# Layer-0 adaLN parts as column-tiled products, and attention outputs in two column halves

## The chip, the cores and the metric

The kernel runs on one core of one Trainium2 chip. Its metric is the device time of one execution in microseconds (us), the median of several runs. Engine names: TensorE (PE; its weight loads are shown as PEld), VectorE (DVE), ScalarE (ACT), GpSimd (POOL), SyncE (SP, which here only starts loads).

## The reference

The model is a trunk of two layers on 512 latent tokens and 256 context tokens of width 1024. What matters here is layer 0: its adaLN parameters and its neighbourhood attention.

```python
silu_c = jax.nn.silu(c)
silu_cc = jax.nn.silu(c_ctx)
for i in range(DEPTH):
    mod_lat = (silu_c @ ada_w[i] + ada_b[i])[:, None, :]
    mod_ctx = (silu_cc @ ada_w[i] + ada_b[i])[None, None, :]
    sh1, sc1, g1, sh2, sc2, g2 = jnp.split(mod_lat, 6, axis=-1)
    csh1, csc1, cg1, csh2, csc2, cg2 = jnp.split(mod_ctx, 6, axis=-1)
    h_lat = modulate(rmsnorm(x, norm_g[i, 0]), sh1, sc1)
    ...
    x = x + g1 * rmsnorm(y_lat, norm_g[i, 1])
    h = modulate(rmsnorm(x, norm_g[i, 2]), sh2, sc2)
...
p = jax.nn.softmax(jnp.concatenate([s_nb, s_cx], axis=-1), axis=-1)
o = (jnp.einsum('bhrqk,brkhd->brqhd', p_nb, v_blk)
     + jnp.einsum('bhrqc,bchd->brqhd', p_cx, v_ctx))
```

Two conditioning vectors, one for latent tokens and one for context tokens, are multiplied with a 1024 x 6144 matrix per layer. The context tokens have an attention of their own with the same keys and values (`context_attention`, 8 heads of width 64).

## The kernel before

Most products run as three fp32r products of split operands (a high and a low part). The stages of layer 0 are the setup and first normalization, spatial gating (`sgu`), attention, the output projection with the residual, and the MLP (`ffn`); layer 1 has retention and a second MLP.

**adaLN.** Four pieces of the first shift and scale are made at the start by `ada_first` (L166): four blocks of 128 rows of the matrix are multiplied side by side, the conditioning vectors as stationary operand 32 columns wide (`c32`), each in its own group of 32 output partitions. The remaining twelfths of layer 0 and all of layer 1, called halves (512 columns of the 6144), are made by `ada_half` (L233). A half loads four blocks of weights (512 KB each, tag `raw`, three buffers shared with other weights). VectorE multiplies each weight row by its conditioning value and adds into an accumulator per stream (latent, context): 8 operations a stream. The accumulators `acc` start from a memset by GpSimd and the bias row, loaded on GpSimd's queue. They are then split, and TensorE sums over the partitions: for gates with a matrix of ones (`ag`), after which VectorE multiplies by the norm weights into a gate tile; for shifts and scales with a selector (`ac`), a copy of the two rows, and four small transposes (`at`).

These halves are generators. `self.bg()` (L220) advances the first of the list `self.jobs` by one step; a step ends at a `yield`. `sgu` calls it six times, `attention` three times while it projects the first pair of heads, and then at every second tile of its loop (L810-811). Layer 0's list (L1693) holds halves 4 and 5 (the attention gate) and 6 to 9 (shift and scale of the MLP). Halves 10 and 11 are made in the MLP stage.

**Attention.** `attention` (L762) walks over 40 tiles, 8 heads with 5 tiles each: four of 128 latent queries, and one of the 256 context queries. For a tile, `score` (L902) makes the scores on TensorE, and VectorE and ScalarE make the softmax. Two tiles later `weigh` (L968) transposes the weights (`pt`, 128 x 512) and ScalarE copies them (`pt_all`, or `pcT` for the context). After the fourth latent tile of a head, six fp32 products with the values (`o`, 64 output partitions, 512 query columns) follow at once; after the context tile, two (`oc`, 256 columns). ScalarE and VectorE split the outputs out of PSUM into `at`. Between these stand the projections of the next pair of heads (`fills`).

PSUM tiles have tags: A with four banks, B with two (scores), C with two. C serves `pt`, `o`, `oc`, the transposed values `vn`, and the adaLN tiles. TensorE, like each engine, works through its queue in order; the order of the queues is set by a scheduler that follows the program's order as priority.

Of the kernel before, what the change touches and what calls it, by code (L numbers as in the profile page):

```python
# [8 lines left out]
F32 = mybir.dt.float32  # L9
# [4 lines left out]
ALU = mybir.AluOpType  # L14
AX = mybir.AxisListType

P = 128
# [51 lines left out]
class Trunk:  # L69
# [66 lines left out]
    def setup(self):  # L136
# [10 lines left out]
        self.ng = self.const("ng", [P, 64], a["ng_col"])  # L147
        self.ones = self.cp.tile([P, P], F32R, name="ones", tag="ones")
# [84 lines left out]
    def ada_half(self, l, half, streams, gate=None, away=False, fine=False):  # L233
        S, V, T, G = self.S, self.V, self.T, self.G
        m, h = divmod(half, 2)
        acc = []
        for s in range(streams):
            t = (self.lp if s else self.bp).tile([P, 512], F32, name=f"acc{l}{half}{s}", tag=f"acc{s}", bufs=1)
            G.memset(t, 0.0)
            G.dma_start(t[0:1], self.a["adab_row"][l * 12 + half : l * 12 + half + 1])  # L240
            acc.append(t)
# [65 lines left out]


# [453 lines left out]
    def attention(self, y, final):  # L762
        a = self.a
        with ExitStack() as ctx:
# [7 lines left out]
            n, lag = len(tiles), 2  # L772
# [8 lines left out]
            for i in range(n + lag):  # L781
# [23 lines left out]
                if i >= lag:  # L805
                    h2, b2 = tiles[i - lag]
                    self.weigh(h2, b2, pairs[h2 // 2], heads[h2])
# [160 lines left out]
    def weigh(self, h, b, pr, hd):  # L968

        S, V, T = self.S, self.V, self.T  # L970
        pt_all, sc = self.pt_all, hd[b]
        rows = slice(64 * (h % 2), 64 * (h % 2) + 64)
        at = pr["at"]
        vc = lambda i: pr["vn"][:, i, rows]
        pt = self.ps(f"pt{h}{b}", "C", (P, 4, P))
        if b < 4:
            for i in range(4):
                T.transpose(pt[:, i, :], sc[:, i * P : (i + 1) * P], self.ident)
            S.copy(pt_all[:, b], pt)
            if b < 3:  # L980
                return
            po = self.ps(f"o{h}", "C")[:64]
            flat = pt_all.rearrange("p a b q -> p (a b) q")
            T.matmul(po, vc(4), pt_all[:, :, 2, :], start=True, stop=False)
            T.matmul(po, vc(5), pt_all[:, :, 3, :], start=False, stop=False)
            T.matmul(po[:, 0:256], vc(1), flat[:, 1:5:3, :], start=False, stop=False)
            T.matmul(po[:, 128:384], vc(2), flat[:, 5:9:3, :], start=False, stop=False)
            T.matmul(po[:, 256:512], vc(3), flat[:, 9:14:4, :], start=False, stop=False)
            T.matmul(
                po.rearrange("p (a q) -> p a q", a=4)[:, 0:4:3, :], vc(0), flat[:, 0:13:12, :], start=False, stop=True  # L990
            )
            src = po.rearrange("p (a r l) -> p r a l", a=4, r=8)
            ov = [x[rows, 0:512].rearrange("p (r a l) -> p r a l", r=8, a=4) for x in at]
            self.split(ov[0], ov[1], src)
            return
        s2 = sc.rearrange("p (b c) -> p b c", b=2)
        for kt in range(2):
            for i in range(2):
                T.transpose(pt[:, 2 * kt + i, :], s2[:, i, kt * P : (kt + 1) * P], self.ident)
        pcT = self.t2k(f"pcT{h}")  # L1000
        S.copy(pcT, pt.rearrange("p k q -> p (k q)"))
        po = self.ps(f"oc{h}", "C")[:64, 0:256]
        for kt in range(2):
            T.matmul(po, vc(4 + kt), pcT[:, kt * 256 : kt * 256 + 256], start=(kt == 0), stop=(kt == 1))
        self.split(at[0][rows, 512:768], at[1][rows, 512:768], po)


# [657 lines left out]
    def build(self):  # L1665
# [19 lines left out]
        with ExitStack() as ctx:  # L1685
# [7 lines left out]
            self.jobs = [self.ada_half(0, h, 2, g1) for h in (4, 5)] + [self.ada_half(0, h, 2) for h in (6, 7, 8, 9)]  # L1693
# [132 lines left out]
```

## Time and profile before

| | |
|---|---|
| median of 3 runs | 1916.56 us (1914.06 to 1920.36) |
| profiled execution, its own time | 1919.05 us |
| its span | 1917.3 us |
| TensorE clock granted, mean | 0.975 |
| HBM read and written | 191.81 MB, 39.85 MB |

The profile is of one execution. A row of a timeline gives start, duration, engine, line, operation, the written and the read tiles, shape and count. Durations of TensorE records include the way through the array, so successive records overlap; what an instruction occupies is read from start to start. All rows carry line L61, because a helper there records every operation; tiles tell the rows apart. A row of waits gives the waiting engine and tile, whom it waited for, the total, the count and the longest.

### The profile page before, as it was taken

Reading aid. Unit: us, or ns where it says so; the run is one execution under the profiler, and the core shown is the slowest. Engines: PE = TensorE matmul, PEld = TensorE weight load, DVE = VectorE, ACT = ScalarE, POOL = GpSimd, SP = SyncE. Lnnn points to the kernel's source line nnn. Section 1 sums busy time; section 2 is a strip of 40 time slices with the busy share of each in tenths; the row PEclk is TensorE's granted clock in tenths of the full one; section 3 lists DMA queues with packets and bytes.
Section 4 is the critical chain, followed back from the end, with each engine's and each line's share of the span. In section 5 each row is a group of like instructions: output and inputs, shape, how many; then the busy total and the mean of one; then the engine's idle time right before and its main releaser. Section 6 shows DMA issues by size and latency. Waiting matters only on the chain. (4 is left out here: it accounts for less than half of the span.)

```text
span 1917.3 us, 28690 instructions
## 1 busy us (share of the span) xinstructions
PE 1799.9 (94%) x10928; PEld 1600.1 (83%) x10928; DVE 1397.0 (73%) x2334; ACT 1019.0 (53%) x1822; POOL 338.7 (18%) x471
## 2 busy tenths in 40 slices
PE   6998989889999999999979999999999989999997
PEld 4886767569989899998869889988999779889986
DVE  4834777779977777877877666676655689788877
ACT  4523545666555555555565434434444467566763
POOL 2102223130122222222021110011001100122221
PEclk9998989989999999999999999999999989999999
DMA  8323332232577778776633413331421225777773
GB/s 309 116 72 105 94 102 72 70 129 69 178 169 154 178 153 171 145 166 138 232 137 121 125 49 113 110 104 51 132 67 56 99 72 154 186 183 181 185 174 101
DMA packets 83978, 250.31 MB, mean 131 GB/s; under 512 B 11136, under 2 KB 12672, under 8 KB 83840
## 3 DMA queue, kind: packets, MB, share of 16 engines
q1 hardware_dynamic: 56960, 199.00, 31.6%
q0 software_dynamic: 26304, 49.36, 15.3%
q8 instruction: 86, 1.41, 0.3%
q14 instruction: 52, 0.43, 0.1%
q10 hardware_dynamic: 576, 0.11, 0.0%
HBM read 191.81 MB, written 39.85 MB: 121 GB/s over the span
## 5 line engine op out<-in xcount | busy, mean ns | idle before, releaser
L61 DVE SCALAR_TENSOR_TENSOR acc<-ar,cs,acc 128x512 f32<-128x512 f32 x256 | 189.5, 758 | 48.4 <-DMA ar<-in_adaw 27.6
L61 DVE SCALAR_TENSOR_TENSOR cv<-pre,cw,cv 128x769 f32<-128x769 f32 (+1 forms) x176 | 152.5, 880 | 7.9 <-ACT cv L61 7.4
L61 ACT ACTIVATE cv<-pre,cw 128x770 f32<-128x770 f32 (+1 forms) x88 | 81.0, 923 | 39.9 <-DVE pre L61 39.1
L61 POOL DMA_DIRECT2D yf<-yp x64 | 54.4, 850 | 269.8 <-ACT yp L61 238.6
L61 POOL DMA_DIRECT2D yd<-yp x54 | 45.9, 862 | 194.0 <-ACT yp L61 187.6
L61 ACT COPY yp<-wf 128x512 f32<-128x512 f32 x118 | 67.9, 577 | 21.2 <-PE wf L61 20.8
L61 ACT ACTIVATE pre<-px 128x256 f32<-128x256 f32 (+2 forms) x160 | 54.3, 365 | 44.7 <-PE px L61 44.3
L61 POOL DMA_DIRECT2D yd<-ypg x54 | 44.7, 851 | 155.4 <-ACT ypg L61 152.9
L61 POOL TENSOR_SCALAR rrr<-rmv 128x2 f32<-128x2 f32 x16 | 3.0, 190 | 357.2 <-DVE rmv L61 357.2
L61 ACT ACTIVATE g<-cv 128x770 fp32r<-128x770 f32 (+1 forms) x44 | 32.5, 738 | 28.2 <-DVE cv L61 28.0
L61 PE MATMUL px<-hs,wd 128*128 128x384 f32 x240 | 45.4, 337 | 0.3 <-DVE pre L61 0.3
L61 PEld LDWEIGHTS px<-hs,wd 128*128 128x128 f32 x240 | 42.3, 188 | 2.2 <-DVE pre L61 0.8
L61 DVE TENSOR_TENSOR g<-cv,g 128x770 fp32r<-128x770 f32 (+1 forms) x44 | 36.1, 821 | 7.2 <-ACT g L61 6.6
L61 ACT ACTIVATE pre<-py 128x384 f32<-128x384 f32 (+1 forms) x40 | 17.4, 436 | 44.5 <-DVE cv L61 25.4
L61 DVE TENSOR_TENSOR pre<-pre,pz 128x256 f32<-128x256 f32 (+1 forms) x60 | 20.8, 370 | 26.1 <-PE pz L61 25.9
L61 ACT ACTIVATE cv<-cv 128x770 f32<-128x770 f32 (+1 forms) x44 | 32.7, 743 | 13.0 <-DVE cv L61 12.9
L61 POOL TENSOR_TENSOR tm<-slab,mask 128x256 f32<-128x256 f32 (+1 forms) x32 | 29.6, 954 | 54.3 <-DVE sst L61 54.2
L61 PEld LDWEIGHTS px<-hs 128*128 128x128 f32 x240 | 32.0, 197 | 8.0 <-DVE pre L61 6.9
L61 PE MATMUL px<-hs 128*128 128x256 f32 x240 | 33.6, 291 | 5.1 <-DVE pre L61 5.1
L61 ACT ACTIVATE sc<-sc,sst 128x512 f32<-128x512 f32 x32 | 23.0, 720 | 28.1 <-DVE sc L61 28.0
L61 DVE TENSOR_TENSOR cv<-cv 128x770 f32<-128x770 f32 (+1 forms) x44 | 36.1, 821 | 2.5 <-ACT cv L61 1.5
L61 ACT COPY ypg<-wf 128x512 f32<-128x512 f32 x54 | 30.8, 577 | 8.8 <-PE wf L61 8.7
(2607 smaller groups left out, 6859.2 us busy)
## 6 DMA issues: line engine op xcount, KB each, us to landing
ar<-in_adaw SPq DMA_DIRECT2D x96, 512.0 KB, 4.2
yf<-yp POOLq DMA_DIRECT2D x64, 256.0 KB, 4.0
yd<-yp POOLq DMA_DIRECT2D x54, 256.0 KB, 5.0
yd<-ypg POOLq DMA_DIRECT2D x54, 256.0 KB, 4.7
fin<-xd SPq DMA_DIRECT2D x10, 512.0 KB, 6.3
xd<-xd SPq DMA_DIRECT2D x8, 512.0 KB, 3.3
xn<-in_x SPq DMA_DIRECT2D x6, 512.0 KB, 8.1
ngr<-in_norm_g POOLq DMA_DIRECT2D x12, 256.0 KB, 3.8
```

Of the source, the lines that this page charges most:

```text
L61: r = f(*p, **k)
```

## The change

1. `ada_packed` takes the place of `ada_half` for the six halves of layer 0 that run in `sgu` and `attention`. TensorE multiplies the weights in fp32, four blocks of 128 rows side by side in four column groups of 32, twice. ScalarE copies the packed result, and the bias row is loaded into partition 2 of the copy. For gates, a full-width fp32 product with a selector (`rows`, made in the setup) sums the groups and the bias; for shifts and scales, four transposes and a sum on VectorE do it. A gate half has four steps and a tail, a shift or scale half three and a tail.
2. The accumulators of the halves that stay with `ada_half` are in the pool of their stage.
3. The value products of a head are five pairs, the left 256 queries in output partitions 0 to 63 and the right 256 in 64 to 127; the context products are two pairs of 128 queries. Each half is split out separately.
4. `weigh` returns these products, and the loop issues them one tile later, before the next transposes.

```diff
+        self.rows = []
+        for i in range(2):
+            v = self.cp.tile([P, 1], F32, name=f"rowv{i}", tag=f"rowv{i}")
+            V.tensor_reduce(
+                out=v, in_=self.ident.rearrange("p (j c) -> p c j", j=4)[:, i, :], axis=AX.X, op=ALU.add
+            )
+            V.tensor_tensor(out=v, in0=v, in1=self.ident[:, 2:3], op=ALU.add)
+            row = self.cp.tile([P, P], F32, name=f"row{i}", tag=f"row{i}")
+            V.tensor_copy(row, v.broadcast_to([P, P]))
+            self.rows.append(row)
...
-            t = (self.lp if s else self.bp).tile([P, 512], F32, name=f"acc{l}{half}{s}", tag=f"acc{s}", bufs=1)
+            t = self.xp.tile([P, 512], F32, name=f"acc{l}{half}{s}", tag=f"acc{s}", bufs=1)
...
+    def ada_packed(self, l, half, streams, gate=None, away=False):
+        S, V, T, G = self.S, self.V, self.T, self.G
+        m, h = divmod(half, 2)
+        ps = self.ps(f"ad{l}{half}", "C")
+        for pair in range(2):
+            for kp in (2 * pair, 2 * pair + 1):
+                raw = self.bp.tile([P, 1024], F32, name=f"ar{l}{half}{kp}", tag="raw", bufs=3)
+                self.load(raw, self.ada_unit_src(l, half, kp))
+                for kk in range(2):
+                    k = 2 * kp + kk
+                    j = k % 4
+                    T.matmul(
+                        ps[32 * j : 32 * j + 32],
+                        self.c32[:, k, :],
+                        raw[:, kk * 512 : kk * 512 + 512],
+                        start=(pair == 0),
+                        stop=(pair == 1),
+                    )
+            yield
+        mr = self.t2k(f"mr{l}{half}")
+        S.copy(mr, ps)
+        G.dma_start(mr[2:3], self.a["adab_row"][l * 12 + half : l * 12 + half + 1])
+        ngr = None
+        if m in (2, 5):
+            ngr = self.t2k(f"ngr{l}{half}")
+            row = l * 4 + (1 if m == 2 else 3)
+            G.dma_start(ngr, self.a["norm_g"][row : row + 1, h * 512 : h * 512 + 512].broadcast_to([P, 512]))
+        yield
+        if m in (2, 5):
+            for s in range(streams):
+                pg = self.ps(f"ag{l}{half}{s}", "C")
+                T.matmul(pg, self.rows[s], mr, start=True, stop=True)
+                dst = gate[s][:, h * 512 : h * 512 + 512]
...
+                    V.tensor_tensor(out=dst, in0=pg, in1=ngr, op=ALU.mult)
+                if s == 0:
+                    yield
+            return
+        pt = self.ps(f"at{l}{half}", "C", (P, 4, P))
+        for i in range(4):
+            T.transpose(pt[:, i, :], mr[:, i * P : (i + 1) * P], self.ident)
+        md = self.bp.tile([P, 4, 2], F32, name=f"md{l}{half}", tag="mt", bufs=2)
+        V.tensor_reduce(out=md, in_=pt.rearrange("p b (j c) -> p b c j", j=4)[:, :, 0:2, :], axis=AX.X, op=ALU.add)
...
+        V.tensor_tensor(out=to, in0=md.rearrange("p b s -> p s b"), in1=two(pt[:, :, 2]), op=ALU.add)
+        if m not in (0, 3):
+            V.scalar_tensor_tensor(
+                out=to, in0=to, scalar=1.0, in1=two(self.ng[:, gi : gi + 4]), op0=ALU.add, op1=ALU.mult
+            )
...
-            for i in range(n + lag):
+            for i in range(n + lag + 1):
...
-                if i >= lag:
+                if out:
+                    out()
+                    out = None
+                if lag <= i < n + lag:
                     h2, b2 = tiles[i - lag]
-                    self.weigh(h2, b2, pairs[h2 // 2], heads[h2])
+                    out = self.weigh(h2, b2, pairs[h2 // 2], heads[h2])
...
+            steps = (
+                (4, pt_all[:, 0:2, 2, :], 4, pt_all[:, 2:4, 2, :], slice(0, 256)),
+                (5, pt_all[:, 0:2, 3, :], 5, pt_all[:, 2:4, 3, :], slice(0, 256)),
+                (1, flat[:, 1:5:3, :], 3, flat[:, 9:14:4, :], slice(0, 256)),
+                (0, one(0), 2, one(8), slice(0, 128)),
+                (2, one(5), 0, one(12), slice(128, 256)),
+            )
+            for n, (k0, x0, k1, x1, c) in enumerate(steps):
+                for r, k, x in ((0, k0, x0), (64, k1, x1)):
+                    T.matmul(po[r : r + 64, c], vc(k), x, start=(n == 0), stop=(n == 4), skip_group_check=True)
+            for half in range(2):
+                src = po[64 * half : 64 * half + 64, 0:256].rearrange("p (a r l) -> p r a l", a=2, r=8)
+                ov = [
+                    x[rows, 0:512].rearrange("p (r a l) -> p r a l", r=8, a=4)[:, :, 2 * half : 2 * half + 2, :] for x in at
+                ]
+                self.split(ov[0], ov[1], src)
...
+            for kt in range(2):
+                for half in range(2):
+                    c = kt * 256 + half * P
+                    T.matmul(
+                        po[64 * half : 64 * half + 64, 0:P], vc(4 + kt), pcT[:, c : c + P], start=(kt == 0), stop=(kt == 1)
+                    )
+            for half in range(2):
+                c = slice(512 + half * P, 512 + half * P + P)
+                self.split(at[0][rows, c], at[1][rows, c], po[64 * half : 64 * half + 64, 0:P])
...
-            self.jobs = [self.ada_half(0, h, 2, g1) for h in (4, 5)] + [self.ada_half(0, h, 2) for h in (6, 7, 8, 9)]
+            self.jobs = [self.ada_packed(0, h, 2, g1) for h in (4, 5)] + [self.ada_packed(0, h, 2) for h in (6, 7, 8, 9)]
```

More of the change, by code (lines that the diff above doesn't have):

```diff
@@ L306, in ada_half @@
                 )
+    def ada_packed(self, l, half, streams, gate=None, away=False):
[31 more added lines that the diff above has]
+                dst = gate[s][:, h * 512 : h * 512 + 512]
+                if away:
+                    g = self.t2k(f"ga{l}{half}{s}")
+                    V.tensor_tensor(out=g, in0=pg, in1=ngr, op=ALU.mult)
+                    G.dma_start(dst, g)
+                else:
+                    V.tensor_tensor(out=dst, in0=pg, in1=ngr, op=ALU.mult)
[7 more added lines that the diff above has]
+        V.tensor_reduce(out=md, in_=pt.rearrange("p b (j c) -> p b c j", j=4)[:, :, 0:2, :], axis=AX.X, op=ALU.add)
+        ab = self.ab[l, 0 if m < 2 else 1]
+        gi = (l * 4 + (0 if m < 2 else 2)) * 8 + h * 4
+        two = lambda x: x.unsqueeze(1).broadcast_to([P, 2, 4])
+        to = ab[:, :, 1 if m in (0, 3) else 0, h * 4 : h * 4 + 4]
+        V.tensor_tensor(out=to, in0=md.rearrange("p b s -> p s b"), in1=two(pt[:, :, 2]), op=ALU.add)
[3 more added lines that the diff above has]
+            )
@@ L771, in attention @@
             tiles = [(h, b) for h in range(8) for b in (0, 1, 2, 3, 4)]
-            n, lag = len(tiles), 2
+            n, lag, out = len(tiles), 2, None
             fills = self.project_pair(0, pairs[0])
@@ L974, in weigh, with products @@
         vc = lambda i: pr["vn"][:, i, rows]
+        def products(h):
+            po = self.ps(f"o{h}", "C")
+            flat = pt_all.rearrange("p a b q -> p (a b) q")
+            one = lambda i: flat[:, i : i + 1, :]
+            steps = (
[14 more added lines that the diff above has]
+                self.split(ov[0], ov[1], src)
         pt = self.ps(f"pt{h}{b}", "C", (P, 4, P))
@@ L980, in weigh @@
             if b < 3:
[L981 to L995, printed above, removed]
+                return None
+            return lambda: products(h)
         s2 = sc.rearrange("p (b c) -> p b c", b=2)
@@ L1001, in weigh, with context @@
         S.copy(pcT, pt.rearrange("p k q -> p (k q)"))
[L1002 to L1005, printed above, removed]
+        def context():
+            po = self.ps(f"oc{h}", "C")
+            for kt in range(2):
[7 more added lines that the diff above has]
+                self.split(at[0][rows, c], at[1][rows, c], po[64 * half : 64 * half + 64, 0:P])
+        return context
     def retention(self, y, final):
```

## The prediction

> **What bounds the kernel now.** I read the page first, then the busy time by stretch, then TensorE's waits inside the stretch that the change touches.
>
> ```profile
> span 1917.3 us, 28690 instructions
> ...
> PE 1799.9 (94%) x10928; PEld 1600.1 (83%) x10928; DVE 1397.0 (73%) x2334; ACT 1019.0 (53%) x1822; POOL 338.7 (18%) x471
> ```
>
> TensorE is busy for 94% of the span, so over the whole kernel only work taken off TensorE, or idle time in front of it, can shorten anything. VectorE's 73% is an average; what it costs must be read where it makes TensorE wait. The busy time by stretch gives the spatial gating stage (57 to 157 us) and the attention stage with its loop (157 to 381 us):
>
> ```profile
> core 0: us, PE busy (x) PEld busy (x) DVE busy (x) ACT busy (x) POOL busy (x), PEclk, DMA share, GB/s
> 57.00:157.00 100.00, 97.27 (x571) 84.13 (x571) 53.17 (x88) 36.70 (x63) 8.98 (x18) 1.00 0.29 93
> ...
> 157.00:381.00 224.00, 197.47 (x1085) 150.99 (x1084) 162.24 (x396) 115.79 (x266) 56.73 (x70) 0.95 0.29 89
> ```
>
> In the gating stage TensorE is busy for 97.27 of 100 us: whatever is added there lengthens the stage. In the attention loop it is idle for 224 - 197.47 = 26.5 us, and VectorE, at 162 of 224 us, is the second load. TensorE's own waits in that stretch say whom it waits for:
>
> ```profile
> PE ag L61 <- DVE al L61: 9.5, 1, 9.5
> PE py L61 <- ACT vt L61: 5.2, 2, 3.8
> PE o L61 <- ACT ptall L61: 3.7, 4, 1.3
> PE s L61 <- ACT sc L61: 2.5, 2, 1.6
> PE pt L61 <- DVE sc L61: 2.2, 1, 2.2
> ```
>
> The columns are the total, the times and the longest. These five make 23.1 of the 26.5 us, and the largest is a wait of the adaLN job itself.
>
> **Value and context products in two halves.** Three rows of TensorE's timeline price them: a block of value products with what follows it, and a block of context products.
>
> ```profile
> 222.66 3.66 PE L61 MATMUL o<-ptall,vn 128*64 128x512 f32 x12
> 226.25 0.66 PE L61 MATMUL pt<-ident,sc 128*128 128x128 f32 x4
> 226.66 0.36 PE L61 MATMUL s<-ka,q 128*128 128x256 f32 x1
> ...
> 227.58 1.08 PE L61 MATMUL oc<-pcT,vn 128*64 128x256 f32 x4
> 228.59 0.66 PE L61 MATMUL pt<-ident,sc 128*128 128x128 f32 x4
> ```
>
> An fp32 product shows as two records. The block of one head holds two products of 512 columns and four of 256, which is 16 records' worth of 256 columns in 226.25 - 222.66 = 3.59 us, or 0.224 us for a record of 256 columns. After the change a head has five pairs: three of 256 columns (two records each) and two of 128. If the two halves of a pair run at the same time, that is 3 x 2 + 2 x 2 x 0.5 = 8 such records, 1.79 us; the saving is 1.8 us a head, 14.4 us for eight. Whether they do can be seen from a product that the kernel already tiles by columns, the first adaLN parts:
>
> ```profile
> 29.72 1.07 PE L61 MATMUL ad<-ar,c 128*32 128x256 f32 x16 [0.34 <-ACT xT L61]
> 30.73 0.66 PE L61 MATMUL ht<-ident,xn 128*128 128x128 f32 x4
> ```
>
> Sixteen records of 256 columns take 30.73 - 29.72 = 1.01 us, not 16 x 0.224 = 3.6 us: four column groups do run side by side. I take the same for two. The context block, 228.59 - 227.58 = 1.01 us for four records, of which 0.9 is work, becomes half of that work: 0.45 us saved a head, 3.6 us for eight. Together -18.0 us. The bounds are -18 and 0, the latter if halves queue behind each other.
>
> That row also holds the price of entering and leaving a tiled block: 1.01 us is four steps of 0.224 and 0.11 more. On this point the Trainium skill (TensorEngine Tiling (Array Packing), Tiling Modes) speaks against the change: switching the tiling mode drains TensorE. The trace agrees in kind, with 0.11 us a block. Without that rule the twelve new blocks below would cost 1.3 us less in all, with it nothing changes in my sum, which uses 1.01 as it stands.
>
> Evacuation doubles in number: the two halves of each output are split separately.
>
> ```profile
> L61 ACT ACTIVATE at<-o x8: 588/590/592, 226.4 to 377.8; 64x512 fp32r<-64x512 f32 x8
> L61 DVE TENSOR_TENSOR at<-o,at x8: 682/684/686, 227.0 to 379.2; 64x512 fp32r<-64x512 f32 x8
> L61 ACT ACTIVATE at<-oc x8: 363/377/377, 228.7 to 380.3; 64x256 fp32r<-64x256 f32 x8
> L61 DVE TENSOR_TENSOR at<-oc,at x8: 408/417/418, 229.1 to 381.3; 64x256 fp32r<-64x256 f32 x8
> ```
>
> A value output costs ScalarE 2 x 0.377 instead of 0.590 and VectorE 2 x 0.417 instead of 0.684; a context half of 128 columns costs between half of and all of the 256-column time. Over eight heads that is at most 4.3 us more on ScalarE (8 x (0.164 + 0.377)) and 4.5 us on VectorE. ScalarE is busy for 116 of 224 us in the loop, so I put it at nothing; uncovered it would be those 4 us.
>
> **The adaLN parts.** Six halves of layer 0 change; the others keep their path, with only their accumulators in another pool, which I cost at nothing. Removed from the stretch:
>
> ```profile
> L61 DVE SCALAR_TENSOR_TENSOR acc<-ar,cs,acc x96: 722/745/1360, 62.6 to 332.0; 128x512 f32<-128x512 f32 x96
> L61 ACT ACTIVATE ah<-acc x12: 619/632/634, 88.1 to 354.6; 128x512 fp32r<-128x512 f32 x12
> L61 DVE TENSOR_TENSOR al<-acc,ah x12: 673/691/1384, 88.8 to 356.3; 128x512 fp32r<-128x512 f32 x12
> ...
> 175.14 0.40 PE L61 MATMUL ag<-ah,ones 128*128 128x512 f32 x1
> 175.37 0.40 PE L61 MATMUL ag<-al,ones 128*128 128x512 f32 x1
> ```
>
> VectorE loses 96 x 0.745 + 12 x 0.691 = 80 us, ScalarE 12 x 0.632 = 7.6 us less six copies of the packed result. TensorE loses 8 summing products for the gates and 16 for the shifts and scales, each 175.37 - 175.14 = 0.23 us: 5.5 us. It gains, per half, two tiled blocks. A block is four products of 512 columns in four groups, as many column steps as the row of sixteen above, so 1.01 us; twelve blocks are 12.1 us. It gains four full-width fp32 products of 512 columns for the gates, 4 x 0.224 = 0.90 us each: 3.6 us. The sixteen transposes of 128 columns stand for sixteen of two columns; four take 226.66 - 226.25 = 0.41 us in the loop and I let the two sets cancel (the other bound: 1.6 us more). Net: +10.2 us on TensorE. Six job steps lie in the gating stage: all of half 4 and both blocks of half 5, so there four blocks and two gate products less four summing products, 4.0 + 1.8 - 0.9 = +4.9 us, uncovered; the other 5.3 us fall into the attention stage.
>
> The six small VectorE operations in the setup (two selector tiles) wait for the identity's load; VectorE is idle early in the kernel, where the inputs are still arriving, and I cost them at nothing, at most 1 us.
>
> **The waits.** The largest of TensorE's waits in the loop, that of ag for al, has these two rows of the timeline about it, the last work on the keys and the first score products:
>
> ```profile
> 183.16 1.59 POOL L61 CAST kb<-kb 64x768 fp32r<-64x768 f32 x2
> ...
> 190.03 0.41 PE L61 MATMUL s<-ka,q 128*128 128x256 f32 x1
> ```
>
> The summing product stood in TensorE's queue ahead of ready projection work, waiting for a split of an accumulator; behind it the projection ran to 190 us, and then the first scores. Next late, once it is gone, are the keys: GpSimd's second cast ends at 184.75 us. So I count 190.03 - 184.75 = 5.3 us, not 9.5. The value products' wait for the copy of the transposed weights (3.7 us) goes whole, since they are now issued a tile later, when the copy is long done; what is late next is the same tile's softmax, which has two tiles of lead. The other three waits, 5.2 + 2.5 + 2.2 = 9.9 us, hang on ScalarE and VectorE queues in which accumulations stood; I take half, 5 us, between bounds of 0 and 9.9. Sum: -14 us.
>
> Against this stand new waits. Before, VectorE waited for the adaLN loads and bias rows; now TensorE reads the loads itself, and a product that waits holds up everything behind it in order. The bias row goes through GpSimd's queue after the copy, and the gate product waits for it.
>
> ```profile
> DVE acc L61 <- DMA ar<-in_adaw: 5.6, 3, 2.7
> DVE acc L61 <- DMA acc<-in_adab_row: 4.6, 2, 3.7
> ...
> SPq L61 <- DVE acc L61: 65.9, 13, 14.1
> ```
>
> If TensorE inherited both, it would lose 10.2 us; if scores and projections fill the time, nothing. I take 4, since job steps stand two tiles apart. The last row is SyncE's queue held by accumulations that still read a buffer (in a stretch that reaches back to 140 us): weights and bias slabs queue behind it. Released by a 1 us block instead of four accumulations, it gives the loads more lead.
>
> **Sum.** -18.0 + 10.2 - 14 + 4 = -17.8 us. The profiled execution took 1919.05 us (span 1917.3 and 1.75 around it); the sum against it is 1901. It lies 2.5 us above the median of the runs, 1916.56, so for a median I say 1899.
>
> **Rivals.** First, slower: the bank becomes the bound. The packed product holds one of the two PSUM banks that the transposed weights and the outputs use, from its first block to its copy, one to two job steps. With one bank left a transposition can't start before the last copy ends:
>
> ```profile
> 217.15 0.60 PE L61 MATMUL pt<-ident,sc 128*128 128x128 f32 x4
> ...
> 217.88 0.61 ACT L61 COPY ptall<-pt 128x512 f32<-128x512 f32 x1
> ```
>
> That is 218.49 - 217.15 = 1.34 us for a tile instead of 0.41, and with the products' own evacuation some 1.3 us lost a tile. Five halves in the loop, two steps of two tiles each: 5 x 4 x 1.3 = 26 us, and the sum becomes +8, 1925 us. It decides if the copy comes a whole step after the second block and no projection fills the gap; were it one step, 13 us, and the result is 1912. The same page of the Trainium skill (Performance Considerations, PSUM Bottleneck) says that tiling speeds up TensorE and not the evacuation, which may become the bottleneck: this rival by rule. Against it speaks that the jobs have ended after 20 of the 30 steps that the two stages offer, and that projections fill the loop's first parts. Chance 0.15.
>
> Second, the halves don't overlap: -18 falls away, 1917 us, no change. The row of sixteen speaks against it. 0.05.
>
> Third, the waits stay, passed on to ScalarE's chain through the softmax, and only -7.8 + 4 is left: 1913. 0.10.
>
> Fourth, VectorE was pacing the whole loop: with 80 us gone the 26.5 us of idle all go and no new wait comes. -18.0 + 10.2 - 26.5 = -34: 1882. For it speaks VectorE's 162 us. 0.15.
>
> The forecast keeps 0.55, with 1889 to 1909 as its own range.
>
> **How the numbers follow.** A measurement of this kernel can tell about 0.3% (5.8 us) from no change. Faster by more: 0.55 + 0.15 and half of the third case, 0.75. Same: the second and the other half, 0.10. Slower: 0.15. The range runs from the fourth rival's 1882 to 1915, past the third and the milder first.
>
> **What would show it.** Right: value blocks near 1.9 us a head, twelve tiled blocks near 1 us, no wait for an accumulator's split around 177 us, the gating stage 5 us longer, the loop about 23 us shorter, VectorE there near 100 us. Wrong: value blocks still above 3 us; TensorE waiting for adaLN loads, the bias row or an evacuation by more than 10 us in the loop; or the stage after the loop no earlier than before.

## The result, and the profile after

The changed kernel takes 1896.48 us in the median, against 1914.06 us for the kernel before on the same chip. The ratio is 0.9907 with a 95% interval of 0.9885 to 0.9930, which is -17.8 us (-22.0 to -13.4). The profiled execution of the changed kernel took 1894.09 us. One of the changed kernel's seven executions was slow (2507.56 us at a granted clock of 0.653); the ratio leaves it out, the median of seven does not.

The head of its page, the same two lines as of before:

```profile
span 1892.3 us, 28961 instructions
...
PE 1796.2 (95%) x11104; PEld 1596.4 (84%) x11104; DVE 1328.8 (70%) x2250; ACT 1015.1 (54%) x1828; POOL 320.6 (17%) x451
```

VectorE is 68 us less busy, TensorE 4 us. That says little yet. The busy time by stretch is cut for both kernels at the same two places in the work: the first projection product of attention, and the first main product of the MLP. So the three rows are gating, attention with its output projection, and everything from the MLP on. First the kernel before:

```profile
core 0: us, PE busy (x) PEld busy (x) DVE busy (x) ACT busy (x) POOL busy (x), PEclk, DMA share, GB/s
57.00:152.41 95.41, 92.68 (x551) 80.47 (x551) 49.69 (x86) 34.46 (x61) 8.98 (x18) 1.00 0.27 88
152.41:484.44 332.03, 294.26 (x1558) 237.79 (x1558) 250.54 (x522) 182.17 (x396) 71.32 (x95) 0.94 0.29 94
484.44:1917.30 1432.86, 1373.05 (x8552) 1255.55 (x8551) 1070.85 (x1679) 773.65 (x1318) 247.81 (x332) 0.98 0.52 136
```

Then the changed kernel, with the same columns:

```profile
57.00:157.73 100.73, 99.92 (x595) 83.24 (x594) 33.87 (x63) 34.72 (x62) 8.44 (x16) 1.00 0.28 95
157.73:468.02 310.29, 285.04 (x1699) 234.46 (x1699) 197.15 (x456) 180.14 (x402) 55.20 (x81) 0.96 0.30 95
468.02:1892.30 1424.28, 1370.98 (x8552) 1251.84 (x8551) 1071.30 (x1679) 771.50 (x1318) 249.21 (x332) 0.98 0.52 137
```

Gating ends 5.3 us later (157.73 against 152.41). The middle stretch is 332.03 - 310.29 = 21.7 us shorter; 9.2 of them are less busy time on TensorE, 12.5 less idle time. VectorE is busy there for 197 us instead of 251. The last stretch is 8.6 us shorter, although the change touches little in it: the accumulators of the halves made there lie in another pool, and GpSimd's queue has another order, but TensorE's 8552 records are the same. A second profiled execution of the kernel before (below) reaches the MLP at 483.04 us and takes 1431.3 us from there. So the traces show 15.0 to 16.4 us gained up to the MLP and 7.0 to 8.6 us behind it; whether the change caused the second part is not shown.

TensorE's waits in the changed kernel from 57 to 381 us (total, times, longest); the first row lies behind the loop, which ends here at 364 us:

```profile
PE ht L61 <- DVE ysg L61: 3.6, 1, 3.6
PE s L61 <- POOL kb L61: 2.0, 1, 2.0
...
PE ag L61 <- DMA mr<-in_adab_row: 0.6, 1, 0.6
PE o L61 <- ACT ptall L61: 0.4, 1, 0.4
...
PE ad L61 <- DMA ar<-in_adaw: 0.3, 1, 0.3
```

The wait of 9.5 us for the accumulator's split is gone, and nothing of its size has come. The value products wait 0.4 us instead of 3.7. The waits that TensorE takes over from VectorE, for the adaLN loads and the bias row, are 0.3 and 0.6 us.

The same stretch of TensorE's timeline as was shown of before:

```profile
219.61 1.07 PE L61 MATMUL ad<-ar,c 128*32 128x512 f32 x8
220.61 0.39 PE L61 MATMUL s<-ka,q 128*128 128x256 f32 x1
...
221.04 1.95 PE L61 MATMUL o<-ptall,vn 128*64 128x256 f32 x20
222.93 0.39 PE L61 MATMUL s<-ka,q 128*128 128x256 f32 x1
...
227.52 0.66 PE L61 MATMUL oc<-pcT,vn 128*64 128x128 f32 x8 [0.20 <-ACT pcT L61]
```

A value block occupies 222.93 - 221.04 = 1.89 us instead of 3.59, and an adaLN block of four column groups 220.61 - 219.61 = 1.00 us: both as forecast, where the products of a block follow each other without a break. Some blocks are broken up, which is taken up below.

**The head of attention** holds the largest single gain. In the kernel before, TensorE's last products ahead of the wait, and those behind it:

```profile
177.25 0.28 PE L61 MATMUL py<-h0a,wv0h 128*128 128x256 f32 x1
187.08 0.80 PE L61 MATMUL ag<-al,ones 128*128 128x512 f32 x1 [9.55 <-DVE al L61]
...
189.81 0.41 PE L61 MATMUL py<-h0a,wv0l 128*128 128x256 f32 x1
190.03 0.41 PE L61 MATMUL s<-ka,q 128*128 128x256 f32 x1
190.24 0.41 PE L61 MATMUL s<-kb,q 128*128 128x256 f32 x1
```

and its granted clock behind the wait (the number after the GpSimd column is PEclk):

```profile
187.00:189.00 2.00, 1.92 (x8) 1.83 (x9) 1.35 (x3) 0.00 (x0) 1.02 (x2) 0.50 0.17 57
189.00:191.00 2.00, 2.00 (x11) 2.00 (x11) 0.03 (x1) 0.90 (x1) 0.00 (x0) 0.50 0.05 9
```

The wait cost more than its 9.55 us: for some 4 us after it the clock was 0.50, and a product of 256 columns came every 0.21 us (190.24 - 190.03) instead of every 0.12 us. In the changed kernel:

```profile
184.51 0.28 PE L61 MATMUL s<-ka,q 128*128 128x256 f32 x1
186.78 0.38 PE L61 MATMUL s<-kb,q 128*128 128x256 f32 x1 [2.00 <-POOL kb L61]
187.00 0.28 PE L61 MATMUL s<-ka,q 128*128 128x256 f32 x1
187.12 0.28 PE L61 MATMUL s<-kb,q 128*128 128x256 f32 x1
```

The keys are next late, as forecast, but only by 2.00 us, and the clock stays up (0.12 us from product to product). From the first projection to the first score product it is 184.51 - 157.73 = 26.8 us instead of 37.6; to the first product that reads the cast keys, 186.78 - 157.73 = 29.1 instead of 37.8, that is 8.8 us less.

### The profile page after: what moved, and what is told of

Its sections match the earlier page's. It is cut to its first block, busy times and chain, and to the rows that moved or that the text cites. A ratio compares the mean times of both kernels' runs of the same rounds, so it can differ in the third digit from the quotient of the medians.

```text
span 1892.3 us, 28961 instructions
## 1 busy us (share of the span) xinstructions
PE 1796.2 (95%) x11104; PEld 1596.4 (84%) x11104; DVE 1328.8 (70%) x2250; ACT 1015.1 (54%) x1828; POOL 320.6 (17%) x451
## 3 DMA queue, kind: packets, MB, share of 16 engines
q0 software_dynamic: 25952, 48.83, 15.1%
## 5 line engine op out<-in xcount | busy, mean ns | idle before, releaser
L61 DVE SCALAR_TENSOR_TENSOR acc<-ar,cs,acc 128x512 f32<-128x512 f32 x160 | 118.1, 750 | 27.7 <-DMA ar<-in_adaw 18.1
L61 PE MATMUL ad<-ar,c 128*32 128x256 f32 (+1 forms) x224 | 26.7, 515 | 10.4 <-DMA ar<-in_adaw 9.8
L61 DVE CUSTOM_DVE_ANT_0 sc<-s,tm 128x256 f32<-128x256 f32 x32 | 13.4, 420 | 32.6 <-PE s L61 23.5
L61 POOL TENSOR_TENSOR tm<-slab,mask 128x256 f32<-128x256 f32 (+1 forms) x32 | 24.4, 793 | 65.2 <-DVE sst L61 65.0
```

Source lines behind the costliest of these rows:

```text
L61: r = f(*p, **k)
```

## The experiments

The theory after the result: the value and context halves overlap and bring nearly all that they were forecast to bring; the adaLN parts cost TensorE work, and pay for it with the waits at the head of attention. The rivals: the gain is the later issue and not the overlap; the accumulations on VectorE paced the whole loop, so that every packed half pays; a PSUM bank is short. In the expectations, A stands for the prediction's terms, B for the reading of the two traces, and C and D for readings that were formed as runs came in. All differences are against the kernel before in the same series of runs, worked out from the ratio; brackets hold the 95% interval.

One accounting serves all of them. Each trace was cut into slices of 3 us at the stage bounds used above. Idle is the slices' length less TensorE's busy time; "slow" is its busy time multiplied by (1 - granted clock), summed; "work" is the rest, the work at full clock. (Some records can be missing, so a difference of a microsecond means nothing.)

| kernel | gating: length, work | attention to MLP: length | work | idle | slow | MLP to end: length | work | idle | slow |
|---|---|---|---|---|---|---|---|---|---|
| before | 95.4, 92.7 | 332.0 | 280.6 | 37.8 | 13.6 | 1432.9 | 1355.8 | 59.8 | 17.2 |
| before, again | 97.0, 93.5 | 329.1 | 280.1 | 35.9 | 13.2 | 1431.3 | 1355.4 | 58.4 | 17.5 |
| changed | 100.7, 99.9 | 310.3 | 274.6 | 25.3 | 10.5 | 1424.3 | 1356.7 | 53.3 | 14.3 |
| adaLN part alone | 100.3, 99.2 | 324.1 | 288.9 | 25.2 | 10.1 | 1423.5 | 1354.9 | 56.3 | 12.4 |
| attention part alone | 97.5, 93.1 | 316.7 | 266.7 | 35.6 | 14.3 | 1428.3 | 1355.1 | 57.0 | 16.1 |
| halves, issued at once | 96.2, 92.8 | 317.2 | 270.4 | 34.3 | 12.5 | 1423.6 | 1355.1 | 54.1 | 14.5 |
| later issue alone | 96.3, 92.6 | 327.9 | 279.8 | 36.6 | 11.5 | 1428.5 | 1355.5 | 58.3 | 14.6 |
| halves in turn | 99.5, 98.6 | 325.9 | 289.1 | 25.1 | 11.7 | 1428.4 | 1356.7 | 56.0 | 15.7 |
| packed, issued at once | 100.0, 99.6 | 318.0 | 277.8 | 30.4 | 9.7 | 1425.0 | 1355.4 | 54.6 | 14.9 |
| halves 4, 5 accumulated | 96.6, 93.4 | 319.2 | 275.8 | 32.4 | 10.9 | 1438.3 | 1356.7 | 62.9 | 18.7 |
| halves 6 to 9 accumulated | 100.5, 99.9 | 310.1 | 266.0 | 29.0 | 15.1 | 1432.0 | 1356.1 | 61.1 | 14.8 |
| half 4 accumulated | 97.7, 96.8 | 308.4 | 274.1 | 24.6 | 9.7 | 1435.7 | 1357.4 | 63.3 | 14.9 |
| longer hold of the bank | 96.4, 94.6 | 311.6 | 277.9 | 22.1 | 11.6 | 1435.3 | 1356.7 | 58.7 | 20.0 |
| gate halves in gating | 109.9, 98.5 | 302.6 | 269.5 | 24.1 | 9.0 | 1438.5 | 1356.0 | 65.0 | 17.5 |

**The kernel before, once more.** No edit; one execution.

> The kernel before, unchanged, for one more trace. It shows how far two executions of the same instructions differ stage by stage. Theory: the stages up to the first MLP agree within 2 us, and the later stages, 1430 us long, by up to 8 us, which is what the traces of the other runs differ by there although their queues are the same. Rival: the first stages differ as much, and no stage time of a single trace can be read to better than 5 us.

Measured: 1916.05 us. Its first projection stands at 153.95 us and its first MLP product at 483.04, against 152.41 and 484.44; the MLP to the end takes 1431.3 against 1432.9. So two traces of one kernel differ by up to 3 us in a stretch here (332.0 against 329.1 us in the middle one), and a smaller difference between two single traces says nothing. Each row of the table is one trace.

**The adaLN part alone.** The kernel before, with `ada_packed`, its selector rows and accumulator pool; `attention` and `weigh` as before.

```diff
-            self.jobs = [self.ada_half(0, h, 2, g1) for h in (4, 5)] + [self.ada_half(0, h, 2) for h in (6, 7, 8, 9)]
+            self.jobs = [self.ada_packed(0, h, 2, g1) for h in (4, 5)] + [self.ada_packed(0, h, 2) for h in (6, 7, 8, 9)]
```

> Only the adaLN part of the change (packed products for six halves, accumulators in the stage's pool); attention as before. Theory A, the terms of the prediction: TensorE gains 10.2 us of work, the waits give back 5.3 + 5 and cost 4, so about 4 us slower than before. Theory B, from the trace of after, where the first score product comes 5.5 us earlier although the gating stage ends 5.3 us later: the relief of VectorE is worth more than the work it costs TensorE, so 3 to 8 us faster than before.

Measured: 1910.62 us against 1914.33, ratio 0.9977, -4.4 us [-7.7 to -1.1]. A falls: the parts pay for themselves, as B said. The table says how: in the middle stretch TensorE has 8.3 us more work (288.9 against 280.6) and 12.6 us less idle time; gating has 6.5 us more work and, with less idle time, grows by 4.9 us. One of the new waits does appear here:

```profile
PE ad L61 <- DMA ar<-in_adaw: 4.9, 2, 4.7
```

**The attention part alone.** The kernel before, with the changed `attention` and `weigh`; the adaLN halves as before.

```diff
+                if out:
+                    out()
+                    out = None
+                if lag <= i < n + lag:
                     h2, b2 = tiles[i - lag]
-                    self.weigh(h2, b2, pairs[h2 // 2], heads[h2])
+                    out = self.weigh(h2, b2, pairs[h2 // 2], heads[h2])
```

> Only the attention part (two column halves, issued a tile later); adaLN as before. Theory A: 18.0 us of TensorE work and the 3.7 us wait go, 22 us faster than before. Theory B: the accumulations still stand in VectorE's queue and hold the loop, so part of the work saved turns into idle time of TensorE: 9 to 14 us faster.

Measured: 1897.64 us, ratio 0.9921, -15.1 us [-19.3 to -10.9]. A's 22 us fall, and B's 9 to 14 lie in the interval, but not for B's reason: work in the middle stretch falls by 13.9 us, and idle time does not rise but falls by 2.2 us (0.3 against the second trace of before). The wait at the head stays:

```profile
PE ag L61 <- DVE al L61: 9.7, 1, 9.7
```

**Halves, issued at once.** The kernel before with the changed `weigh`, whose products are called where they were.

```diff
-                    self.weigh(h2, b2, pairs[h2 // 2], heads[h2])
+                    out = self.weigh(h2, b2, pairs[h2 // 2], heads[h2])
+                    if out:
+                        out()
```

> Only the two column halves, issued at once as before; adaLN as before. Theory A: 18 us faster than before, with the wait for the copied weights still there. Theory B: 6 to 12 us faster.

Measured: 1899.63 us, ratio 0.9920, -15.3 us [-21.2 to -9.4]. A's 18 us lie in the interval, and so does part of B's range. The kernel cannot be told from the one with the later issue: without the packed parts, the halves bring all of the gain that can be measured.

**The later issue alone.** The kernel before with its full-width products, returned by `weigh` and called a tile later.

```diff
-            po = self.ps(f"o{h}", "C")[:64]
+            def products():
+                po = self.ps(f"o{h}", "C")[:64]
...
+            return products
```

> Only the later issue: full-width value and context products, one tile later; adaLN as before. Theory A: the 3.7 us wait for the copy goes, 3.7 us faster than before. Theory B: the scheduler already fills that wait with other work and a wait elsewhere takes its place, within 2 us of before.

Measured: 1915.58 us, ratio 1.0009, +1.7 us [-0.6 to +3.8]. A's -3.7 falls. The wait that the later issue was to remove does get shorter (1.7 us instead of 3.7). TensorE's idle time in the middle stretch is 36.6 us, between the 37.8 and 35.9 of the two traces of before, so the 2 us don't show in the sum:

```profile
PE ag L61 <- DVE al L61: 9.8, 1, 9.8
PE py L61 <- ACT vt L61: 4.2, 2, 4.0
PE pt L61 <- DVE sc L61: 2.9, 2, 1.5
...
PE o L61 <- ACT ptall L61: 1.7, 2, 1.2
```

**Halves in turn.** The changed kernel with the same pairs of products, but both halves in output partitions 0 to 63, one half after the other.

```diff
-            for n, (k0, x0, k1, x1, c) in enumerate(steps):
-                for r, k, x in ((0, k0, x0), (64, k1, x1)):
-                    T.matmul(po[r : r + 64, c], vc(k), x, start=(n == 0), stop=(n == 4), skip_group_check=True)
+            for r in (0, 64):
+                for n, (k0, x0, k1, x1, c) in enumerate(steps):
+                    k, x = (k1, x1) if r else (k0, x0)
+                    T.matmul(po[0:64, 4 * r + c.start : 4 * r + c.stop], vc(k), x, start=(n == 0), stop=(n == 4), skip_group_check=True)
```

> The changed kernel, but both column halves of a product go to the same output partitions, one half after the other: the same number of products, copies and splits, without the overlap. Theory A (overlap on TensorE is the whole gain of the attention part): the 15 us that the halves alone gave go, so about 3 us faster than before and 15 us slower than the changed kernel. Rival (issue order, shorter holds of the PSUM bank and smaller evacuations give part of it): 8 us faster than before or better.

Measured: 1913.96 us against 1916.09, ratio 0.9995, -1.0 us [-4.0 to +2.1]. The same twenty records, counted and evacuated as in the changed kernel, take twice as long when both halves write the same output partitions:

```profile
224.49 3.68 PE L61 MATMUL o<-ptall,vn 128*64 128x256 f32 x20
228.09 0.39 PE L61 MATMUL s<-ka,q 128*128 128x256 f32 x1
```

That is 3.60 us instead of 1.89, and 289.1 us of work in the middle stretch instead of 274.6. Idle times are equal (25.1 and 25.3). So the overlap is worth 14.5 us of TensorE work, and it goes into the time: -17.8 us against -1.0, 16.8 by the medians.

**Packed parts, products issued at once.** The changed kernel with the products called in their own tile.

```diff
-                    out = self.weigh(h2, b2, pairs[h2 // 2], heads[h2])
+                    now = self.weigh(h2, b2, pairs[h2 // 2], heads[h2])
+                    if now:
+                        now()
```

> The changed kernel with the value and context products issued at once, not a tile later; everything else as in the changed kernel. Theory (the later issue is worth nothing, as alone): within 2 us of the changed kernel. Rival (with VectorE relieved, TensorE comes to the products before the copy is done, and the later issue begins to count): 4 us slower than the changed kernel, 14 us faster than before.

Measured: 1902.37 us, ratio 0.9939, -11.7 us [-15.5 to -7.7], some 6 us more than the changed kernel; the intervals overlap. The middle stretch is 7.7 us longer, 5.1 of them idle. Two of its waits:

```profile
PE ad L61 <- DMA ar<-in_adaw: 4.6, 2, 2.7
...
PE pt L61 <- ACT ptall L61: 2.1, 2, 1.9
```

The 6 us are nearer to the rival's 4 than to the theory's 2, but with overlapping intervals neither is shown. What the two traces show is that the blocks wait for their loads by 0.3 us with the later issue and by 4.6 us here, and that there is 3.2 us more work (277.8 against 274.6).

**Half 4 accumulated.** The changed kernel with one half back on VectorE; the selector is read with a stride of zero instead of from a copy.

```diff
-            self.jobs = [self.ada_packed(0, h, 2, g1) for h in (4, 5)] + [self.ada_packed(0, h, 2) for h in (6, 7, 8, 9)]
+            self.jobs = [self.ada_half(0, 4, 2, g1), self.ada_packed(0, 5, 2, g1)]
+            self.jobs += [self.ada_packed(0, h, 2) for h in (6, 7, 8, 9)]
```

> The changed kernel with half 4 accumulated on VectorE as before (its products run in the gating stage), the other five packed; the selector for the gates is read with a zero stride instead of from a full tile. Theory C (the gating stage is bound by TensorE and VectorE has room there): two tiled blocks and two gate products go and four summing products come, 2.9 us less than the changed kernel, about 20 us faster than before. Theory D (VectorE's relief is the gain): no faster than the changed kernel, 15 to 18 us faster than before.

Measured: 1896.50 us, ratio 0.9911, -17.1 us [-21.3 to -12.8]: the same as the changed kernel. Its trace reaches the MLP 4.9 us earlier (463.10 against 468.02) and takes 11.4 us more from there (1435.7 against 1424.3). Undecided between C and D.

**Halves 6 to 9 accumulated.** The changed kernel with 4 and 5 packed and 6 to 9 on VectorE; the selector as in the run above.

> The changed kernel with halves 6 to 9 accumulated on VectorE as before, halves 4 and 5 packed; the selector as in the run above. Theory C (the gain of the packed parts is the wait at the head of the attention stage, which belongs to half 5; in the loop they cost TensorE eight blocks less sixteen summing products, 4.4 us): 2 to 5 us faster than the changed kernel, 20 to 23 us faster than before. Theory D (the gain is VectorE's relief in the loop): 4 to 8 us slower than the changed kernel, 10 to 14 us faster than before.

Measured: 1900.65 us, ratio 0.9923, -14.8 us [-19.2 to -10.5]. C's -20 and more falls; D's 10 to 14 lie in the interval. Beside the changed kernel TensorE has 8.6 us less work in the middle stretch, and loses it again: 3.7 us to idle time and 4.6 us to the lower clock. Packing these four halves is worth 3 us by the medians; the intervals overlap.

**Halves 4 and 5 accumulated.** The other way round: 4 and 5 on VectorE, 6 to 9 packed. The accumulators are in their old pools and the selector tiles are gone, as in the kernel before.

> The changed kernel with halves 4 and 5 accumulated on VectorE as before, halves 6 to 9 packed; accumulators in their old pools, no selector tiles. Theory C: the gating stage becomes 3.6 us shorter and the wait of 9 to 10 us for the split at the head of the attention stage returns: 5 to 7 us slower than the changed kernel, about 11 us faster than before. Theory D: within 2 us of the changed kernel.

Measured: 1909.82 us, ratio 0.9975, -4.8 us [-7.5 to -2.1]: 13 us slower than the changed kernel, where C said 5 to 7 and D at most 2. The wait at the head of attention is back, and the lower clock behind it:

```profile
PE ag L61 <- DVE al L61: 8.8, 1, 8.8
```

```profile
186.30:188.30 2.00, 1.97 (x9) 1.46 (x13) 0.69 (x1) 0.46 (x2) 1.76 (x3) 0.50 0.69 238
188.30:190.30 2.00, 2.00 (x10) 0.53 (x3) 0.00 (x0) 0.00 (x0) 0.50 (x1) 0.50 0.40 157
190.30:192.30 2.00, 2.00 (x12) 2.00 (x11) 0.69 (x1) 0.00 (x0) 0.00 (x0) 0.50 0.65 170
```

TensorE runs 6 us at half clock. Half 4 alone on VectorE brought no such wait, so it belongs to half 5. But most of the loss lies elsewhere. The two profiled executions differ by 4.8 us up to the MLP and by 14.0 us behind it (62.9 us of idle time and 18.7 us of lost clock instead of 53.3 and 14.3), with the same work and the same order of the queues on TensorE, VectorE, ScalarE and SyncE. GpSimd's order there is that of the kernel before; so it is in the attention part alone, which takes 1428.3 us there, while the gate halves in gating (below) have the changed kernel's order and take 1438.5. Why more is lost behind the MLP's start is open.

Nor is it shown that packing the two gate halves pays by itself. With the changed attention, no half packed gives -15.1 us, halves 4 and 5 alone -14.8, 6 to 9 alone -4.8, and all six -17.8. Packing 6 to 9 without 4 and 5 loses some 10 us ([-7.5 to -2.1] against [-19.3 to -10.9]); packing 4 and 5 alone adds nothing that can be measured. The parts do not add up, and the cause of that is not known.

**A longer hold of the bank.** The changed kernel with one more step between the last block of a half and its copy, so that the packed product holds its bank for a step longer. In the traces the four halves of the loop hold it from the first block to the end of the copy for 88.5 us in all instead of 65.9; half 7 gains most (32.3 us instead of 15.8), and half 8 holds it for less (12.2 instead of 14.6).

```diff
             yield
+        yield
         mr = self.t2k(f"mr{l}{half}")
```

> The changed kernel with one more job step between a packed product's second block and its copy, so that it holds one of the two PSUM banks two tiles longer. The rival of the prediction (with one bank left a tile's transposes wait for the last copy, 1.3 us a tile): four halves in the loop, two tiles each, 4 x 2 x 1.3 = 10 us slower than the changed kernel. Theory: transposes and products find a bank in time, and nothing in the changed kernel's trace waits for it by more than 2 us: within 3 us of the changed kernel, 15 to 20 us faster than before.

Measured: 1897.87 us against 1916.58, ratio 0.9899, -19.4 us [-24.5 to -14.0]. The rival of the bank asked for some 10 us more than the changed kernel, and it falls, although only halves 6 and 7 held the bank clearly longer. TensorE's waits for the copy of the weights (`at` behind `ptall`) and for evacuations (`pt` behind `at`) are 2.6 and 2.2 us in all. The Trainium skill (TensorEngine Tiling (Array Packing), Performance Considerations) warns that PSUM evacuation may become the bottleneck of a tiled kernel; by these two waits it does not here.

**All of the gate halves in gating, by accumulation.** Halves 4 and 5 by `ada_half`, and `self.bg()` at every step of gating instead of every second, so that they are finished before attention begins.

```diff
-                    if n % 2:
-                        self.bg()
+                    self.bg()
```

> The changed kernel with halves 4 and 5 accumulated on VectorE, and a job step after every tile of the gating stage instead of every second, so that both gate halves are done before the attention stage begins; halves 6 to 9 packed; no selector tiles. Theory C (the wait for the split at the head of the attention stage was the cost, and VectorE has room in the gating stage): no wait for a split at the head, and TensorE's work in the gating stage falls by four blocks and four gate products less eight summing products, 5.8 us, less two blocks of half 6 that move in: 3 to 5 us faster than the changed kernel, 20 to 23 us faster than before. Rival: the accumulations now hold up VectorE's work on the gating product itself, and the gating stage gains nothing: 15 to 18 us faster than before.

Measured: 1908.80 us, ratio 0.9956, -8.4 us [-11.3 to -5.4]. C falls, and the rival's 15 to 18 too. The idea, to remove the wait at the head without TensorE work, does remove it (the clock stays at 1.00 there), but gating ends 9 us later than in the changed kernel: TensorE, which the changed kernel keeps busy for 99.92 of 100.73 us in gating, is idle for 109.87 - 100.08 = 9.8 us; the largest of its waits there are for VectorE and ScalarE. From the MLP on this execution also took 1438.5 us.

```profile
57.00:166.87 109.87, 100.08 (x587) 84.59 (x586) 57.86 (x100) 36.53 (x64) 10.61 (x21) 0.98 0.38 120
```

```profile
PE ug L61 <- DVE un L61: 3.2, 1, 3.2
PE ag L61 <- ACT ah L61: 2.1, 1, 2.1
```

No version was faster than the changed kernel beyond the intervals.

## Why the prediction was right, point by point

The mechanism of the largest term, halves that overlap, was right and is shown. That the sum agrees to a tenth is luck: its parts were off by up to 8 us, and the errors cancelled. By parts, the forecast was -18.0 for the halves, -3.7 for the later issue and +10.2 - 5.3 - 5 + 4 = +3.9 for the adaLN parts; measured alone, they gave -15.3, +1.7 and -4.4. By kind, the forecast was -7.8 of TensorE work and -10 of waits; from 57 us to the MLP the traces show 1.2 us more work, 14.4 us less idle time and 3.1 us less lost clock. So all of TensorE's work that the halves save goes into the adaLN parts, and what shortens the stretch is the waits and the clock.

- **The value and context products** (forecast -18.0). The block came out at 1.89 us, the forecast 1.79 plus 0.1. The work saved is 13.9 us (attention part alone) to 14.5 us (against halves in turn), and -15 us in the time. The mechanism was right and shown; the size was 3 to 4 us too large. Part of that is blocks that are not whole: in the changed kernel the eight take 17.0 us instead of 8 x 1.89 = 15.1, because two of them have their first product apart from the others and two are held up inside. That doubling the evacuations costs nothing that can be measured held: the time fell by about what TensorE saved.
- **The adaLN work on TensorE** (forecast +10.2, 4.9 of it in gating). In the adaLN part alone it is 14.8 us: 8.3 in the middle stretch and 6.5 in gating. All four gate products ran ahead of the first projection (the last at 127.57 us in the changed kernel), where the working counted two; that makes 4.0 + 3.6 - 0.9 = 6.7 us in gating and leaves 3.5 for the middle stretch. Gating became only 4.9 us longer, as forecast, because idle time there filled up. Of the 4.8 us too much in the middle stretch, some 3 are blocks torn in two. The four column groups ran side by side only where the products followed each other; here is one block in the changed kernel with other work in between:

```profile
262.30 1.04 PE L61 MATMUL ad<-ar,c 128*32 128x512 f32 x2
263.27 0.66 PE L61 MATMUL vn<-ident,vt 128*128 128x128 f32 x4
263.86 1.06 PE L61 MATMUL ad<-ar,c 128*32 128x512 f32 x6
264.85 0.39 PE L61 MATMUL s<-ka,q 128*128 128x256 f32 x1
```

  One product by itself (two records) takes 263.27 - 262.30 = 0.97 us and the other three 264.85 - 263.86 = 0.99: each piece as much as a whole block. Three of the eight blocks in the middle stretch are torn, in the changed kernel as in the adaLN part alone, by other work in the queue or by a wait for a load. The working took twelve whole blocks. The last 2 us no run separates.
- **The head of attention** (forecast -5.3). Here the working was too careful. It held the keys' time fixed and counted only up to their cast. Two things were missed. The keys themselves stood behind accumulations: VectorE's timeline of the kernel before has this (the bracket is its idle time ahead of the row; what it waited for is not named):

```profile
174.57 1.04 DVE L61 SCALAR_TENSOR_TENSOR acc<-ar,cs,acc 128x512 f32<-128x512 f32 x1 [5.74 <-issue]
175.53 0.21 DVE L61 TENSOR_TENSOR kb<-pk,ka 64x64 fp32r<-64x64 f32 x1
```

  The split of the keys (`kb`) stood for 5.74 us behind an accumulation that could not start. And the clock fell to 0.50 after TensorE's wait. Measured, the head is 8.8 us shorter up to the first score that uses the cast keys.
- **The later issue** (forecast -3.7). Wrong as a term of its own (+1.7, interval -0.6 to +3.8): its wait became 2 us shorter and the kernel no faster. Whether it is worth some 6 us together with the packed parts, as the medians say, is not shown.
- **The other waits and the new ones** (forecast -5 and +4). TensorE's idle time in the middle stretch fell by 12.5 us in the changed kernel and the lost clock by 3.1, all waits together (10.6 and 2.7 against the second trace of before); the forecast's net was -10. The new waits are 0.9 us in the changed kernel, but 4.9 and 4.6 us in two of its neighbours: all lie within the bounds of 0 to 10.2, and these kernels differ in what stands in TensorE's queue around the blocks.
- **The rivals.** The bank is refuted by the longer hold, for the two halves that it lengthened. That the halves do not overlap is refuted by halves in turn. That the waits stay is refuted by the waits shown. That VectorE paced the whole loop is refuted too: with 53 us less work on VectorE in the middle stretch 25.3 us of idle time are left, and packing four of the six halves brings 3 us by the medians.
- **What would show it**: the whole value and adaLN blocks, the missing wait at 177 us, and gating 5 us longer all came as stated. The stretch from the first projection to the MLP is 21.7 us shorter; the forecast said about 23 for the loop. VectorE is busy for 112 us from the first projection to 364 us, the forecast said near 100.

## What to carry to other kernels

Two fp32 products of 64 output partitions, side by side, took the time of one here (1.89 us instead of 3.60 for a head), and as TensorE was the bound the kernel kept what that saved. This holds while the products follow each other: a piece of a torn block costs as much as the whole, so a block's products should stand together and start when all their loads are there (not tried here). Look for the one wait that ends last before you count the busy time that you free on another engine, and price it with the lower clock behind it. Try parts together as well as alone: packing halves 6 to 9 without 4 and 5 made this kernel 10 us slower than packing none.

## What the runs showed of the hardware

A wait costs TensorE more than its length. In the kernel before 9.55 us of waiting are followed by 4 us at a granted clock of 0.50, and in the middle stretch 13.6 us of its time go to the lower clock. The Trainium skill (TensorE: Matmul & The Clock Gate, Part 1, What's actually happening) says that the clock is halved after an idle window of about 3.4 us, and that this window runs free of the program. The traces agree on the half. They also show that a gap need not be that long: TensorE waited 2.43 us in the adaLN part alone, and one microsecond after it went on, products of 512 columns, issued every 0.23 us before, came every 0.43 us:

```profile
186.74 0.39 PE L61 MATMUL s<-kb,q 128*128 128x256 f32 x1 [2.43 <-POOL kb L61]
...
187.20 0.39 PE L61 MATMUL pq<-h0a,wq1h 128*128 128x512 f32 x1
187.43 0.40 PE L61 MATMUL pq<-h1a,wq1h 128*128 128x512 f32 x1
...
188.06 0.63 PE L61 MATMUL pq<-h0a,wq1h 128*128 128x512 f32 x1
188.48 0.63 PE L61 MATMUL pq<-h1a,wq1h 128*128 128x512 f32 x1
```

The changed kernel's 2.00 us at the same place left the clock at full; a wait of 2.02 us at 1632.7 us in the same execution was followed by a clock of 1.00 for one microsecond and of 0.56 over the next two. So waits near that length come out at one price or at another.

The stages from the MLP on took 1423.5 to 1438.5 us in the kernels of the table, with 1355 to 1357 us of full-clock work in every one. What differs is idle time (53 to 65 us) and lost clock (12 to 20 us). So a difference of 5 us between two profiled executions proves nothing by itself. Which of those waits set it off was not tried.
